# First retention outputs read while the last pair of gate columns is computed: loads, splits, stores and SBUF places around the start of the sliding-window phase

## The chip, the cores and the metric

The kernel runs on one core of one Trainium2 chip. Its engines work side by side, each in the order of its own queue: TensorE (PE, matmuls into PSUM), VectorE (DVE), ScalarE (ACT), GpSimd (POOL) and SyncE (SP), which only issues DMAs here. ACT and POOL can issue DMAs too. The metric is the device time of one execution in microseconds (us). Before the change the median of three runs is 2251.56 us.

## The reference

One layer of a streaming encoder over 1024 prompt tokens and 64 sample tokens, 1088 in all, with 1024 channels. What matters here is the first sublayer:

```python
rq, rk, rv, rg, sq, sk, sv, ga, gb = in_proj(h, g_attn, w_in)
...  # retention -> ret_o, sliding-window attention -> swa_o
a = (rms_norm(ret_o).astype(ret_g.dtype).reshape(B, S, -1) * jax.nn.silu(ret_g)) @ w_ret_out
b = swa_o.reshape(B, S, -1) @ w_swa_out
return (jax.nn.sigmoid(gate_a) * a + jax.nn.sigmoid(gate_b) * b) @ w_mix_out
```

`gate_b` (the columns `w_gb`) is the last thing that the projection computes. Then come the sliding-window attention (SWA: 16 query heads in 2 groups, a window of own chunk and two earlier chunks of 64 tokens) and the product with `w_ret_out`. Cross attention, a SwiGLU and a last norm follow, and the caches are returned.

## The kernel before

**Precision.** Every large product takes float32 operands split in two: a cast on ACT gives the high part, a subtraction on DVE the low part (`split`, L122 to L124), and three matmuls use them. Work that is "split" therefore always costs one ACT and one DVE instruction.

**Projection with seven products.** The projection handles two blocks of 128 output columns and both halves of the tokens at once (`strassen`, L247). For each such pair the weights `P1` to `P7` are made from two raw tiles (POOL adds, then splits into `wq` tiles, five of them), and PE runs seven products with the operands in the order `B11`, `B21`, `T2`, `T1`, `T3`, `B22`, `T4`. The operands live for the whole projection in two rings of eight slots of [128, 2, 1088] words each: ring 0 holds the two tiles of `T4` in slots 0 and 1, eight half-size staging areas in slots 2 and 3, `B11` in 4 and 5, `T1` in 6 and 7; ring 1 holds `B21` in 0 and 1, `B22` in 2 and 3, `T2` in 4 and 5, `T3` in 6 and 7. After the last pair each slot comes free when its product has been computed. The last pair's results are staged in ring 0's slot 3, the pair's before it in slot 2.

**Gate columns** (`project`, L654 to L664). For each result a DVE multiplication, an ACT sigmoid (L572) and a store into `d_gate` follow. For the swish gate (index 0, which then holds the gated retention outputs) the store is on SP, for the branch gates A and B (indices 1, 2) on ACT's own queue (L658). During most pairs a piece of the memory keys and values is computed as well.

**SWA phase** (`swa`, L871, with `filler`, L1045). A query chunk of 64 tokens and half of the heads make one step; 34 steps are run as a software pipeline in the order weigh, scores, turn (transposes), and between them pieces of dense work from `filler`: four pieces of the last memory values (`w_mv`) and then, for each of eight column blocks of `w_ret_out`, six pieces of 12 matmuls (three token chunks of 384, 384 and 320 columns, each in two halves of the contraction). PE's order is written out by hand (`in_order`). All other engines get their order from a scheduler that simulates the program: instructions traced earlier, or under `high_priority`, go first among those whose inputs and space are ready by its own model. `issue_after(x)` keeps an instruction behind `x` on the same engine's queue.

**Space in SWA.** The eight slots of ring 0 are taken anew as `swin` tiles, from slot 4 on: `flat[0]`, `flat[1]` are `B11`'s, `flat[2]`, `flat[3]` `T1`'s, `flat[4]`, `flat[5]` `T4`'s, `flat[6]`, `flat[7]` the staging areas'. They hold kT and vT (keys and values, 128 x 1216 words), the bias (128 x 1536), two buffers of queries (128 x 2048, for four chunks each), transposed values `vts`, and ten load buffers of 384 columns, `lds`. In ring 1 eight `ret` tiles take the split retention outputs. `operands` (L1055) loads them from `d_gate[0]` chunk by chunk of the tokens, eight loads of 128 x 384 (or 320) a chunk, through `lds`, and splits each. Their loads go on SP behind the `w_mv` loads. The loads of vT go behind the last load of the first chunk (`operand_loaded`), and the second query load (`load_queries(qTs, 4)`) is traced with the first scores. The raw tiles of `w_mv` (two) and of `w_ret_out` share two buffers.

## Time and profile before

| | us |
|---|---|
| runs, median (lowest to highest) | 2251.56 (2247.32 to 2252.81) |
| profiled execution, its own time | 2246.01 |
| its span, first to last instruction | 2244.2 |
| PE busy in the span | 2161.9 |
| mean granted PE clock | 0.988 of full |

A page of the profile shows one execution. Lines such as L123 name a line of the kernel, often that of a helper, so the tiles after it (`ret<-swin`) tell what it works on. "Idle before" an instruction is the time in which its engine had nothing to do, and what ended it. In the timeline views a row has the start, the length, engine, line, operation, output and input tiles and, in brackets, that idle time. DMA issues show on the issuing queue (SPq, ACTq); they land later.

### The profile page before, as it was taken

To read this page: it belongs to the slowest core of one execution; us is meant where nothing else is said; L and a number is where in the kernel's file an instruction comes from. 1 tells how busy PE (TensorE), PEld (TensorE's weight loads), DVE (VectorE), ACT (ScalarE), POOL (GpSimd) and SP (SyncE) were. 2 spreads that over 40 slices of the span, in tenths; PEclk is the share of its full clock that TensorE was granted. 3 is DMA by queue.
4 is the path that set the end of the run, shared out by engine and by line. 5 is a ranking of instruction groups with operands and counts; after the bars stand their busy time and mean duration, and the time that the engine had idled before them with its cause. 6 is when DMAs were issued, how large, how long until landed. Compare 5 with 4: busy or idle time off the path is not lost.

```text
span 2244.2 us, 41644 instructions
## 1 busy us (share of the span) xinstructions
PE 2161.9 (96%) x16374; PEld 2097.0 (93%) x16374; DVE 1602.8 (71%) x2655; ACT 883.9 (39%) x1896; POOL 689.8 (31%) x466
## 2 busy tenths in 40 slices
PE   7899999999999989999999999999999999999996
PEld 6899999999999977779999998999999999999986
DVE  8995878676687568875455565676777777778587
ACT  7333333435444355553233343333222222344343
POOL 1441533342263112220000000015555556434462
PEclk9999999999999989999999999999999999999998
DMA  5433345443545475327343112422342332476233
GB/s 198 161 116 110 111 130 134 130 127 115 172 141 188 144 242 166 111 68 219 118 153 119 38 49 71 133 78 88 122 138 92 102 128 83 151 263 196 75 96 108
DMA packets 182598, 290.84 MB, mean 130 GB/s; under 512 B 40290, under 2 KB 110850, under 8 KB 182402
## 3 DMA queue, kind: packets, MB, share of 16 engines
q1 hardware_dynamic: 177794, 279.26, 39.2%
q10 hardware_dynamic: 4608, 8.91, 1.1%
q8 instruction: 129, 2.11, 0.4%
q14 instruction: 67, 0.55, 0.1%
HBM read 196.95 MB, written 91.16 MB: 128 GB/s over the span
## 4 chain that ended last, share of the span: by engine, by line
PE 80%; DVE 10%; DMA 4%; issue 2%; ACT 2%; POOL 1%; SPq 0%; DVEq 0%; ACTq 0%; POOLq 0%
PE pq L208 15%; PE pq L205 15%; PE pq L206 15%; PE pd L149 8%; PE pd L151 8%; PE pd L150 8%; DVE wq L124 2%; PE pout L992 1%; DMA hl<-d_op 1%; PE pp L976 1%; PE pss L934 1%; DVE T L124 1%; DVE B L124 1%; DMA qs<-d_qkv 1%; PE pk L691 1%
## 5 line engine op out<-in xcount | busy, mean ns | idle before, releaser
L124 DVE TENSOR_TENSOR wq<-raw,wq 128x512 fp32r<-128x512 f32 (+1 forms) x505 | 456.6, 908 | 126.4 <-ACT wq L123 124.2
L123 ACT CAST wq<-raw 128x512 fp32r<-128x512 f32 (+1 forms) x505 | 307.7, 614 | 562.6 <-PE pq L208 266.5
L205 PE MATMUL pq<-T,wq 128*128 128x272 f32 x1832 | 492.5, 289 | 5.6 <-DVE u L252 3.7
L206 PE MATMUL pq<-T,wq 128*128 128x272 f32 x1832 | 492.8, 289 | 0.0
L206 PE MATMUL pq<-B,wq 128*128 128x272 f32 x1592 | 430.1, 290 | 9.7 <-DVE B L124 9.5
L205 PE MATMUL pq<-B,wq 128*128 128x272 f32 x1592 | 428.0, 289 | 11.8 <-ACT wq L123 10.6
L208 PE MATMUL pq<-T,wq 128*128 128x272 f32 x1832 | 384.1, 290 | 3.6 <-DVE wq L124 3.6
L183 POOL TENSOR_TENSOR raw<-raw 128x512 f32<-128x512 f32 (+1 forms) x59 | 82.7, 1402 | 905.9 <-DVE wq L124 623.6
L205 PEld LDWEIGHTS pq<-T,wq 128*128 128x128 f32 x1832 | 346.0, 189 | 6.3 <-DVE u L252 3.7
L206 PEld LDWEIGHTS pq<-T,wq 128*128 128x128 f32 x1832 | 346.0, 189 | 0.3 <-issue 0.3
L208 PE MATMUL pq<-B,wq 128*128 128x272 f32 x1592 | 334.2, 290 | 0.0
L206 PEld LDWEIGHTS pq<-B,wq 128*128 128x128 f32 x1592 | 301.2, 189 | 12.2 <-DVE B L124 11.8
L205 PEld LDWEIGHTS pq<-B,wq 128*128 128x128 f32 x1592 | 300.8, 189 | 12.5 <-ACT wq L123 10.6
L208 PEld LDWEIGHTS pq<-T,wq 128*128 128x128 f32 x1832 | 291.0, 190 | 5.1 <-DVE wq L124 4.4
L208 PEld LDWEIGHTS pq<-B,wq 128*128 128x128 f32 x1592 | 253.5, 190 | 0.5 <-issue 0.3
L252 DVE TENSOR_TENSOR u<-pq,u 128x544 f32<-128x544 f32 x177 | 127.5, 721 | 112.3 <-PE pq L208 111.7
L186 POOL TENSOR_TENSOR raw<-raw 128x512 f32<-128x512 f32 (+1 forms) x59 | 83.1, 1408 | 133.8 <-DVE wq L124 126.2
L563 DVE TENSOR_TENSOR stage<-pq,u 128x544 f32<-128x544 f32 x112 | 80.3, 717 | 27.7 <-PE pq L208 25.3
L962 POOL TENSOR_TENSOR t<-t,den 128x768 f32<-128x768 f32 (+2 forms) x34 | 47.9, 1407 | 167.4 <-DVE nm L950 58.7
L184 POOL TENSOR_TENSOR raw<-raw 128x512 f32<-128x512 f32 (+1 forms) x59 | 88.1, 1494 | 3.7
L189 POOL TENSOR_TENSOR raw<-raw 128x512 f32<-128x512 f32 (+1 forms) x59 | 84.0, 1424 | 4.4
L1438 POOL TENSOR_TENSOR y<-u,y 128x544 f32<-128x544 f32 x38 | 61.9, 1638 | 76.3 <-DVE y L1436 52.0
(370 smaller groups left out, 4647.2 us busy)
## 6 DMA issues: line engine op xcount, KB each, us to landing
hl<-d_op SPq DMA_DIRECT2D x85, 272.0 KB, 4.0
d_qkv<-stage SPq DMA_DIRECT2D x44, 272.0 KB, 2.1
d_op<-stage SPq DMA_DIRECT2D x44, 272.0 KB, 2.1
d_op<-ht SPq DMA_DIRECT2D x44, 272.0 KB, 3.2
raw<-w_gate SPq DMA_DIRECT2D x22, 512.0 KB, 3.4
raw<-w_up SPq DMA_DIRECT2D x22, 512.0 KB, 3.6
d_gate<-stage ACTq DMA_DIRECT2D x32, 272.0 KB, 2.3
raw<-w_down SPq DMA_DIRECT2D x16, 512.0 KB, 4.4
```

Of the source, the lines that this page charges most:

```text
L123: self.last_cast = self.nc.scalar.copy(hi, src).ins
L124: return self.nc.vector.tensor_tensor(out=lo, in0=src, in1=hi.bitcast(F32), op=ALU.subtract).ins
L149: mm(ps, wh, xh, start=start, stop=False)
L150: mm(ps, wh, xl, start=False, stop=False)
L151: self.last_mm = mm(ps, wl, xh, start=False, stop=stop).ins
L184: tt(out=a21, in0=a21, in1=a22, op=add)
L186: tt(out=a11, in0=a22, in1=a11, op=sub)
L189: tt(out=a12, in0=a12, in1=a11, op=sub)
L205: mm(ps[:, c, :HC], w[:, 0, ks], x[:, 0, cs], start=start, stop=False)
L206: mm(ps[:, c, :HC], w[:, 0, ks], x[:, 1, cs], start=False, stop=False)
L208: self.last_mm = mm(ps[:, c, :HC], w[:, 1, ks], x[:, 0, c * HC:(c + 1) * HC], start=False, stop=stop).ins
L252: add = lambda out, a, b: nc.vector.tensor_tensor(out=out, in0=a, in1=b, op=ALU.add)
```

## The change

Five things change. The last pair of gate B columns stores its four results by GpSimd's queue. The `swin` tiles get new uses: kT goes from `B11`'s first slot to `T1`'s first, the bias to `T1`'s second, the transposed values to the staging slot 2, and the load buffers to `B11`'s first slot (five at first) and `T4`'s second (five more after the first chunk). The eight `ret` tiles are put into ring 1's slots in the order `B21`, `T2`, `T3`, `B22`. The first chunk's operand loads no longer have to be behind the `w_mv` loads, and the later chunks' and vT's go behind the bias load; the second query load goes behind the last operand load. The first unit of `w_ret_out` is loaded and split ahead of the second chunk in the order of tracing.

```diff
-                    store = nc.scalar.dma_start if idx else self.store
+                    store = nc.gpsimd.dma_start if (idx, m) == (2, KT - 2) else nc.scalar.dma_start if idx else self.store
...
-            kT, vT = flat[0][:, :KC], flat[5][:, :KC]
-            bias = flat[2][:, :NPAIR * NKEY].rearrange("p (a b) -> p a b", b=NKEY)
+            kT, vT = flat[2][:, :KC], flat[4][:, :KC]
+            bias = flat[3][:, :NPAIR * NKEY].rearrange("p (a b) -> p a b", b=NKEY)
...
-            vts = [flat[4][:, i * P:(i + 1) * P] for i in range(17)] + [flat[0][:, KC + i * P:KC + (i + 1) * P] for i in range(3)]
-            self.lds = [t[:, i * 384:(i + 1) * 384] for t in (flat[3], flat[6]) for i in range(5)]
+            vts = [flat[6][:, i * P:(i + 1) * P] for i in range(17)] + [flat[2][:, KC + i * P:KC + (i + 1) * P] for i in range(3)]
+            self.lds, self.more_lds = ([t[:, i * 384:(i + 1) * 384] for i in range(5)] for t in (flat[0], flat[5]))
...
-                    self.load(bias[e * 64:(e + 1) * 64], src)
+                    self.bias_loaded = self.load(bias[e * 64:(e + 1) * 64], src)
...
-                if hf == 0 and c % 4 == 0 and c + 4 < 17:
+                if hf == 0 and c % 4 == 0 and 0 < c < 13:
                     self.load_queries(qTs, c + 4)
...
-                    with tc.high_priority(), tc.issue_after(self.operand_loaded):
+                    with tc.high_priority(), tc.issue_after(self.bias_loaded):
                         tokens(vT, 1, "cvT")
+                    with tc.issue_after(self.last_operand):
+                        self.load_queries(qTs, 4)
...
-            rets = self.ring_tiles(1, KT, "ret")
+            rets = [self.rings[1].tile(f"ret{k}", slot=i) for k, i in enumerate((0, 1, 4, 5, 6, 7, 2, 3))]
 
             def operands(c0, n):
-                after = self.loaded
+                after = self.bias_loaded
                 for k in range(KT):
                     a = ld()
-                    with tc.issue_after(after):
-                        ins = self.load(a[:, :n], self.d_gate[0][k, :, c0:c0 + n])
-                    if c0 == 0:
-                        self.operand_loaded = ins
+                    with tc.issue_after(after) if c0 else nullcontext():
+                        self.last_operand = self.load(a[:, :n], self.d_gate[0][k, :, c0:c0 + n])
                     self.split(a[:, :n], rets[k][:, 0, c0:c0 + n], rets[k][:, 1, c0:c0 + n])
-
-            for c0, n in CH:
+                if c0 == 0:
+                    self.lds += self.more_lds
+
+            operands(*CH[0])
+            first = self.unit(io["w_ret_out"][0], KT)
+            for c0, n in CH[1:]:
                 operands(c0, n)
...
-                u = self.unit(io["w_ret_out"][m], KT)
+                u = self.unit(io["w_ret_out"][m], KT) if m else first
```

More of the change, by code (lines that the diff above doesn't have):

```diff
@@ L1 @@
 import math
-from contextlib import ExitStack, contextmanager
+from contextlib import ExitStack, contextmanager, nullcontext
 import numpy as np
```

## The prediction

> **What bounds the kernel now.** I read the page first.

> ```profile
> span 2244.2 us, 41644 instructions
> PE 2161.9 (96%) x16374; PEld 2097.0 (93%) x16374; DVE 1602.8 (71%) x2655; ACT 883.9 (39%) x1896; POOL 689.8 (31%) x466
> ```

> TensorE (PE) is busy for 96% of the span, so a change that touches no matmul can only win where PE stands idle or runs at a lowered clock. The busy times by stage show one such place around this change, the seam between the last pair of gate columns and the sliding-window (SWA) phase; the columns are busy us (and instructions) of PE, PEld, DVE, ACT and POOL, then granted PE clock, DMA share and GB/s.

> ```profile
> 800.00:814.20 14.20, 14.20 (x116) 14.05 (x115) 6.29 (x10) 1.97 (x3) 0.00 (x0) 1.00 0.79 228
> 814.20:817.50 3.30, 0.57 (x8) 0.43 (x8) 1.45 (x2) 1.28 (x3) 0.00 (x0) 0.84 0.52 164
> 817.50:823.30 5.80, 5.61 (x24) 5.32 (x25) 5.04 (x13) 5.71 (x16) 0.00 (x0) 0.51 0.92 294
> 826.10:830.00 3.90, 2.40 (x23) 1.58 (x22) 2.92 (x10) 1.69 (x9) 0.00 (x0) 1.00 0.91 317
> 830.00:835.10 5.10, 0.00 (x0) 0.00 (x0) 3.60 (x12) 5.10 (x21) 1.81 (x2) 0.51 0.91 321
> 835.10:838.00 2.90, 2.23 (x6) 1.73 (x7) 2.90 (x6) 2.90 (x7) 0.13 (x1) 0.50 1.00 322
> 838.00:841.00 3.00, 3.00 (x14) 2.18 (x14) 2.83 (x6) 1.75 (x6) 0.00 (x0) 0.62 0.88 263
> 852.30:862.00 9.70, 9.70 (x74) 7.65 (x72) 9.08 (x20) 6.66 (x27) 2.97 (x2) 1.00 0.66 205
> 814.20:852.30 38.10, 25.85 (x162) 21.30 (x162) 31.09 (x76) 27.00 (x85) 3.79 (x4) 0.78 0.90 291
> 862.00:999.00 137.00, 137.00 (x976) 106.34 (x976) 109.39 (x241) 71.71 (x275) 36.69 (x25) 1.00 0.31 97
> ```

> From 814.2 to 852.3 PE is idle for 38.1 - 25.85 = 12.25 us. Before it and from 862 on PE never idles, so what the seam gives up should reach the end one for one. The same seam has DMA at 0.90 of its time and DVE at 31.09 of 38.1. The timeline of PE names what ended the largest gaps; in brackets stands the idle time:

> ```profile
> 817.55 0.58 PE L149 MATMUL pd<-wq,ms 128*128 128x256 f32 x1 [2.78 <-ACT wq L123]
> 829.65 0.33 PE L911 MATMUL pd<-ident,swin 128*128 128x128 f32 x1 [0.80 <-DMA swin<-d_skv]
> 835.14 0.69 PE L149 MATMUL pd<-ret,wq 128*128 128x384 f32 x1 [5.16 <-ACT wq L123]
> 836.77 0.69 PE L151 MATMUL pd<-ret,wq 128*128 128x384 f32 x1 [0.62 <-DVE wq L124]
> ```

> The chain of waits (start, us, what) says why the longest lasts until 835:

> ```profile
> 816.42 0.36 ACTq L658
> 816.94 0.46 issue
> 817.40 1.65 ACT wq L123 x3
> ...
> 820.13 8.16 DMA swin<-d_gate
> 828.31 0.51 ACT ret L123
> ...
> 838.48 6.59 DMA raw<-w_ret_out
> ```

> ACT, in order, sits on the eighth load of a retention output (issued at 820.13, and landed 8.16 us later) with the casts of the first `w_ret_out` unit behind it. SyncE's (SP) queue shows why loads are late:

> ```profile
> 794.79 0.32 SPq L117 DMA_DIRECT2D swin<-d_skv  x1
> ...
> 796.29 0.37 SPq L117 DMA_DIRECT2D swin<-d_sq  x1
> 797.80 3.23 SPq L117 DMA_DIRECT2D raw<-w_mv  x2
> 803.75 1.32 SPq L117 DMA_DIRECT2D swin<-d_rb  x2
> 806.92 12.68 SPq L117 DMA_DIRECT2D swin<-d_gate  x7
> 819.70 0.38 SPq L117 DMA_DIRECT2D swin<-d_sq  x1
> ```

> The space of operand `B11` comes free first (kT goes into it at 794.79), that of `T1` only around 803.75 (the bias goes into it); the load buffers lie behind that. At 819.70 a query load (`d_sq`) stands ahead of the eighth operand load.

> **The change, part by part.** (1) The load buffers take the `B11` tile, so five operand loads can start at 794.8 instead of 806.9, and three more as the first splits free a buffer; the `ret` tiles are numbered by the order in which the products free ring 1 (`B21`, `T2`, `T3`, `B22`). Products end 3.0 us apart, as their evacuations show (805.25, 808.24):

> ```profile
> 805.25 0.72 DVE L252 TENSOR_TENSOR u<-pq,u 128x544 f32<-128x544 f32 x1 [2.26 <-PE pq L208]
> 808.24 0.72 DVE L252 TENSOR_TENSOR u<-pq,u 128x544 f32<-128x544 f32 x1 [2.26 <-PE pq L208]
> ```

> So the eight slots come free between about 798 and 811, and eight casts and eight subtractions fit ahead of 814.2. Their prices in the seam, by group (count, busy us, mean ns):

> ```profile
> L124 DVE TENSOR_TENSOR ret<-swin,ret 128x384 fp32r<-128x384 f32 x16 | 9.6, 629 | 1.6 <-ACT ret L123 1.5
> L123 ACT CAST ret<-swin 128x384 fp32r<-128x384 f32 x16 | 7.3, 507 | 3.5 <-DMA swin<-d_gate 3.5
> ```

> Eight cost DVE 9.6 / 2 = 4.8 us and ACT 7.3 / 2 = 3.7 us. In 800 to 814.2 DVE is busy 6.29 and ACT 1.97 of 14.2, so they lie beside PE at no cost. If that cover failed (a cast waiting on a late load with the evacuation of a product behind it) PE would stop once its three result buffers are full, two products or 6 us later.

> (2) kT moves behind `T1`, from 794.8 to about 803.6, beside the bias at about 805. Bytes that have to land from 794.8 until the first retention matmul, by the shapes of the tiles: kT 0.6 MB, queries 1.05, `w_mv` 1.05, bias 0.8, eight operands 1.57, stores 1.1, vT 0.6, `w_ret_out` 0.5, and up to 1.57 of the next chunk ahead of it: 8.9 MB. At the seam's 291 GB/s that is 30.6 us (until 825.4), at the 334 GB/s of the row below (797.0 to 803.7) 26.6 us.

> ```profile
> DMA packets 1111, 2.24 MB, mean 334 GB/s; under 512 B 206, under 2 KB 334, under 8 KB 1110
> ```

> PE gets to that matmul at about 828.7 (after 826.1 come 2.40 us of work and some 0.7 of a wait between two score tiles, less 0.5 from part 4), so the 5.16 us should go. What could be late next is `w_ret_out`, whose raw buffer is free only after the `w_mv` splits (about 819).

> (3) vT waits for the bias load only, the second query load goes behind the last operand load, `w_ret_out` ahead of the second chunk. That removes the 0.80 us (vT) and 0.62 us (DVE), and SP's stop at 819.70.

> (4) Four stores leave ACT's queue for POOL's. ACT's casts of `w_mv` come 0.5 us earlier (0.36 issue and part of the 0.46 behind it), PE's first gap shrinks from 2.78 to 2.3 us. POOL is idle there:

> ```profile
> 824.87 0.77 POOL L962 TENSOR_TENSOR t<-t,den 128x256 f32<-128x256 f32 x1 [28.85 <-ACT ret L123]
> L658 ACTq DMA_DIRECT2D d_gate<-stage x6: 326/326/359, 781.2 to 816.4; - x6
> DMA to landing us min/median/max: 2.0/2.5/4.8
> ```

> The trace has no store issued by POOL. From below I bound its cost by ACT's 0.33 us and 2.0 us landing, from above by SP's slowest operand load (0.50 us to issue, 8.16 to land). Either way the last lands by 816.4 + 8.7 = 825. Only the second query load waits for it (the gate columns are read much later), and that load comes up on SP after all operand loads; the 16 later ones alone carry 2.9 MB, 8.7 us at 334 GB/s, so hardly before 823. I take nothing; at the upper bound SP stands for 2 us, with later `w_ret_out` units behind it that PE needs six pieces later.

> (5) Clock. After the 5.16 us gap PE runs at 0.50 and 0.62. The work of 835.1 to 841.0 at full clock is 2.23 x 0.50 + 3.00 x 0.62 = 3.0 us of 5.9, so 2.9 us, of which 0.6 is the DVE gap counted above: 2.3 us.

> **Sum** on PE: 5.16 + 0.80 + 0.62 + 0.5 + 2.3 = 9.4 us at most. DVE caps it: 31.09 - 4.8 = 26.3 us of work take 32.2 us at its present share (0.82), 28.1 at the 0.94 of 852.3 to 862: 5.9 to 10.0 us won. DMA too: 38.1 x 291 = 11.1 MB less 1.57 takes 32.7 us at 291 GB/s, 28.5 at 334: 5.4 to 9.6 won. I take 8.0, the middle of DVE's bounds, since DVE is the busiest engine of the seam and its work is what the later steps wait for. The profiled execution took 2246.0 (span 2244.2 and 1.8 around it), 5.6 below the median of the runs shown, so 2238.0 of it means 2251.6 - 8.0 = 2243.6 of the median.

> **The rivals.** (A) The wait only moves: the same bytes are carried by a DMA system busy 0.90 of the seam, and ACT meets the second chunk or `w_ret_out` (the 6.59 us row) where it met the first. Then only 0.5 + 0.8 + 0.6 = 1.9 us remain, 2249.7. For it speaks the DMA share of 0.91 to 1.00 from 817.5 to 838; against it that DMA is at 0.52 from 814.2 to 817.5 and can be filled.

> (B) The first gap no longer halves the clock. Now 817.5 to 823.3 runs at about 0.50 after 2.78 us of idling; with 2.3 us it might stay full, 5.8 / 2 = 2.9 us more, 2240.7. Against it: the clock already fell to a mean of 0.84 within 814.2 to 817.5.
> [...]

> (C) Slower: SP's queue is in order, and kT's three loads are written ahead of the operands with high priority. If they are also ahead in SP's queue, SP stands at them from 794.8 to 803.6 and every load behind them, queries and `w_mv` too, starts up to 8.8 us later, the chain at 820.13 with them. Price 0 to 8.8 us; with the full price and the 1.9 us of A, 2251.6 + 8.8 - 1.9 = 2258.5. It decides from the first load SP issues after 794.8. Against it: at 806.92 seven operand loads stand ahead of a query load written before them whose buffer wasn't free; for it: bias and operands do keep their written order.

> **How the numbers follow.** Forecast 0.57 (own range 2241 to 2247), A 0.20, B 0.10, C 0.13. A measurement of this kernel tells about 0.3% (6.8 us, below 2244.8) from no change. Of the forecast's chance 0.7 lies beyond that: faster 0.40 + 0.10 = 0.50; same 0.17 + 0.20 = 0.37; slower 0.13. The range reaches down to a gain near all that the seam loses (12.25 idle plus half-clock work, some 15 us) and up into C's smaller prices: 2236 to 2254.

> **What would show it.** Operand loads on SP from 794.8 on, eight `ret` casts before 814; the first `ret` matmul near 829 at clock 1.00 with no wait over 1 us; steady PE from about 844 in place of 852; the first gap still there, then 0.50. It is wrong if kT leads SP's queue, if PE has idle time before 814, or if ACT waits on an operand or `w_ret_out` load for 3 us or more after 817.

## The result, and the profile after

| | kernel before | changed kernel |
|---|---|---|
| runs on the same chip, median (lowest to highest), us | 2249.18 (2245.82 to 2255.40), 14 runs | 2256.12 (2252.99 to 2261.21), 14 runs |
| ratio, 95% interval | 1 | 1.0032 (1.0024 to 1.0040) |
| profiled execution, its own time, us | 2246.01 | 2259.77 |

The change makes the kernel slower by 0.32%, 6.9 us of the medians; 2243.6 had been predicted, 8 us faster. The profiled execution of the changed kernel is 13.8 us longer than that of the kernel before, more than the medians say, so the two traces must be cut into stretches before they are compared. These are the header lines of its page:

```profile
span 2258.0 us, 41646 instructions
...
PE 2168.5 (96%) x16374; PEld 2104.1 (93%) x16374; DVE 1600.3 (71%) x2655; ACT 885.4 (39%) x1896; POOL 689.6 (31%) x470
```

As marks I take PE's and DVE's timelines: the last evacuation of the gate columns (L563), the first `ret` matmul, the first 320-column piece of the first `w_ret_out` unit, the last `ret` matmul, the first `swa` matmul (where the merge begins) and the first `xc` matmul after the merge. The table has us from the first mark, one profile in each line:

| | L563 at | first ret | first 320 | last ret | first swa | first xc |
|---|---|---|---|---|---|---|
| before | 814.22 | 20.92 | 42.72 | 219.74 | 219.89 | 413.88 |
| changed | 816.92 | 14.59 | 42.04 | 219.08 | 226.18 | 419.81 |
| changed, second profile | 814.39 | 13.49 | 39.89 | 216.93 | 223.89 | 416.94 |

Three readings follow. The 2.70 us before the first mark lie in code that the change does not touch, and the second profile does not have them. From the end of the merge on the order of work is the same too, and the span left after the last `co` matmul (in the cross attention) is 749.7 to 756.1 us in the thirteen profiles whose marks stand above and below (750.9 before, 756.1 after, 751.5 in the second profile). So of the 13.8 us, 2.7 lie ahead of the first mark and 5.2 behind the merge, in code that both kernels share, and 5.9 between (419.81 against 413.88). What belongs to the change is between: the seam, which wins 0.7 us (2.8 in the second profile) where 8 were forecast, and the step from the last `ret` to the first `swa` matmul, which costs 7.0 us (219.08 to 226.18, against 219.74 to 219.89).

**The seam.** PE's timeline of the changed kernel, only rows with a wait over 0.5 us (idle time in brackets):

```profile
819.65 0.39 PE L149 MATMUL pd<-wq,ms 128*128 128x256 f32 x1 [2.18 <-ACT wq L123]
...
829.98 0.71 PE L934 MATMUL pss<-swin,swin 64*128 64x128 f32 x8 [1.67 <-DVE t L947]
...
842.99 1.06 PE L976 MATMUL pp<-ident,t 128*64 128x128 f32 x4 [6.38 <-POOL t L962]
```

The waits of 0.80, 5.16 and 0.62 us are gone. A new one of 6.38 us stands at the transposes of half (0,1), which need `t` from POOL. The busy times in three stretches (same columns as in the prediction) show the price, PE idle for 6.49 of 15 us and a granted clock of 0.68, while DVE is busy 13.46 of 15:

```profile
815.00:830.00 15.00, 10.81 (x82) 10.08 (x80) 9.52 (x23) 9.63 (x24) 1.69 (x3) 0.89 1.06 306
830.00:845.00 15.00, 8.51 (x45) 7.00 (x46) 13.46 (x40) 13.61 (x48) 1.93 (x3) 0.68 0.94 317
845.00:860.00 15.00, 15.00 (x94) 11.86 (x93) 9.29 (x20) 5.84 (x22) 2.26 (x2) 0.87 0.55 190
```

DVE's timeline says what it was busy with. DVE's part of the half's softmax is the chain L949, L950, L951, L954, L959, L960 on rows of 4 elements; splits (L124) stand between its links:

```profile
830.82 0.41 DVE L949 TENSOR_REDUCE nm<-t 128x4 f32<-128x256 f32 x1
831.15 1.48 DVE L124 TENSOR_TENSOR ret<-swin,ret 128x384 fp32r<-128x384 f32 x3
...
833.22 0.15 DVE L950 TENSOR_TENSOR nm<-nm,sinks 128x4 f32<-128x4 f32 x1
833.28 1.35 DVE L124 TENSOR_TENSOR ret<-swin,ret 128x384 fp32r<-128x384 f32 x3
...
835.22 1.28 DVE L124 TENSOR_TENSOR wq<-raw,wq 128x512 fp32r<-128x512 f32 x2
...
837.56 0.15 DVE L954 TENSOR_TENSOR es<-sinks,nm 128x4 f32<-128x4 f32 x1
...
840.55 0.89 DVE L124 TENSOR_TENSOR ret<-swin,ret 128x320 fp32r<-128x320 f32 x2
...
841.98 0.17 DVE L960 RECIPROCAL den<-den 128x4 f32<-128x4 f32 x1
```

Between 830.82 and 841.98 the engine rests for 0.16 us only, but the splits of the third chunk (128x320) and of the next two `w_ret_out` units are work that PE needs only later, and PE stands for the softmax behind them. ACT's half of each split does the same. The exponentials of the half are done at 837.7 and `es` (L954) is ready at 837.71, but ACT takes it up only at 839.79, behind casts, the first of which had to wait for its load:

```profile
837.49 0.19 ACT L956 ACTIVATION_READ_ACCUMULATOR t<-t,nm 128x1 f32 x1
838.03 1.14 ACT L123 CAST wq<-raw 128x512 fp32r<-128x512 f32 x2 [0.35 <-DMA raw<-w_ret_out]
839.07 0.81 ACT L123 CAST ret<-swin 128x320 fp32r<-128x320 f32 x2
839.79 0.20 ACT L958 ACTIVATE es<-es 128x4 f32<-128x4 f32 x1
```

**The merge.** PE's timeline there has one wait (the second row is the same matmul in the kernel before, without one), and the windows behind it a lowered clock:

```profile
1043.10 1.33 PE L149 MATMUL pd<-swa,wq 128*128 128x384 f32 x3 [6.79 <-ACT swa L123]
```

```profile
1034.11 0.34 PE L149 MATMUL pd<-swa,wq 128*128 128x384 f32 x1
```

```profile
1036.00:1043.00 7.00, 0.31 (x3) 0.04 (x1) 4.60 (x9) 3.83 (x9) 0.00 (x0) 0.80 0.97 321
1043.00:1048.00 5.00, 4.90 (x18) 4.90 (x19) 3.75 (x9) 3.05 (x8) 0.00 (x0) 0.60 0.90 269
```

`merge_swa` retakes ring 0's slots for eight tiles `swa0` to `swa7`, from slot 4 on. So `swa0` lies where `flat[0]` was. The change puts load buffers there, and these serve until the last `d_mix` stores of the SWA phase. Every accumulation of the merge begins with k = 0, so the tile that comes free last is now the one needed first. In the kernel before, the load buffers in use at the end lay in `flat[6]`, which becomes `swa6`, and PE worked on the six tiles ahead of it without a gap.

### The profile page after: what moved, and what is told of

Its sections match the earlier page's. It is cut to its first block, busy times and chain, and to the rows that moved or that the text cites. A ratio compares the mean times of both kernels' runs of the same rounds, so it can differ in the third digit from the quotient of the medians.

```text
span 2258.0 us, 41646 instructions
## 1 busy us (share of the span) xinstructions
PE 2168.5 (96%) x16374; PEld 2104.1 (93%) x16374; DVE 1600.3 (71%) x2655; ACT 885.4 (39%) x1896; POOL 689.6 (31%) x470
## 4 chain that ended last, share of the span: by engine, by line
PE 79%; DVE 10%; DMA 4%; issue 3%; ACT 2%; POOL 1%; SPq 0%; DVEq 0%; ACTq 0%; POOLq 0%
PE pq L208 15%; PE pq L206 15%; PE pq L205 15%; PE pd L149 7%; PE pd L151 7%; PE pd L150 7%; DVE wq L124 2%; PE pout L992 2%; PE pp L976 1%; PE pss L934 1%; DMA hl<-d_op 1%; DVE B L124 1%; DVE stage L563 1%; DVE T L124 1%; DMA ld<-d_swa 1%
## 5 line engine op out<-in xcount | busy, mean ns | idle before, releaser
L124 DVE TENSOR_TENSOR wq<-raw,wq 128x512 fp32r<-128x512 f32 (+1 forms) x505 | 452.6, 900 | 127.2 <-ACT wq L123 125.3
L123 ACT CAST wq<-raw 128x512 fp32r<-128x512 f32 (+1 forms) x505 | 307.6, 614 | 566.7 <-PE pq L208 276.1
L208 PE MATMUL pq<-T,wq 128*128 128x272 f32 x1832 | 383.9, 290 | 3.4 <-DVE wq L124 3.4
L208 PE MATMUL pq<-B,wq 128*128 128x272 f32 x1592 | 335.5, 291 | 0.0
L208 PEld LDWEIGHTS pq<-T,wq 128*128 128x128 f32 x1832 | 291.1, 190 | 4.5 <-DVE wq L124 3.8
L208 PEld LDWEIGHTS pq<-B,wq 128*128 128x128 f32 x1592 | 254.9, 191 | 0.5 <-issue 0.3
L252 DVE TENSOR_TENSOR u<-pq,u 128x544 f32<-128x544 f32 x177 | 127.5, 720 | 107.3 <-PE pq L208 106.6
L563 DVE TENSOR_TENSOR stage<-pq,u 128x544 f32<-128x544 f32 x112 | 80.3, 717 | 25.4 <-PE pq L208 22.8
L962 POOL TENSOR_TENSOR t<-t,den 128x768 f32<-128x768 f32 (+2 forms) x34 | 47.4, 1393 | 146.0 <-DVE nm L950 51.3
```

The lines of the kernel that those rows point to most:

```text
L123: self.last_cast = self.nc.scalar.copy(hi, src).ins
L124: return self.nc.vector.tensor_tensor(out=lo, in0=src, in1=hi.bitcast(F32), op=ALU.subtract).ins
L208: self.last_mm = mm(ps[:, c, :HC], w[:, 1, ks], x[:, 0, c * HC:(c + 1) * HC], start=False, stop=stop).ins
L252: add = lambda out, a, b: nc.vector.tensor_tensor(out=out, in0=a, in1=b, op=ALU.add)
L563: nc.vector.tensor_tensor(out=o, in0=ps, in1=sb, op=ALU.add)
```

## The experiments

All ratios are to the kernel before, with 95% intervals. e1 to e5 shared runs of it (median 2249.9), then e3c, e7, e6 and the second profile (2248.64), then e9, e8 and e6_again (2249.27). Their marks, in us from the last evacuation as above:

| | first ret | first 320 | last ret | first swa | first xc |
|---|---|---|---|---|---|
| e1_swap | 13.41 | 39.38 | 216.31 | 216.45 | 410.38 |
| e2_before_swap | 20.93 | 42.00 | 219.08 | 226.37 | 420.11 |
| e3b_order | 13.96 | 35.08 | 256.88 | 257.03 | 451.02 |
| e3c_splits | 14.17 | 36.43 | 220.89 | 221.03 | 414.96 |
| e9_third | 13.26 | 36.03 | 213.07 | 213.21 | 407.20 |
| e5_actstore | 17.61 | 43.12 | 220.03 | 220.17 | 414.09 |
| e6_unfirst | 16.00 | 37.75 | 214.68 | 214.83 | 408.75 |
| e6_again | 16.00 | 39.70 | 216.74 | 216.89 | 410.87 |
| e7_wfirst | 13.68 | 37.84 | 221.27 | 221.41 | 415.33 |
| e8_third_unfirst | 13.67 | 40.31 | 217.40 | 217.54 | 411.53 |

### e1_swap and e2_before_swap: the place of `swa0`

Both have one line of the merge altered, e1 in the changed kernel and e2 in the kernel before; `swa0` and `swa6` exchange their slots:

```diff
-            swas = self.ring_tiles(0, KT, "swa")
+            swas = [self.rings[0].tile(f"swa{k}", slot=i) for k, i in enumerate((2, 5, 6, 7, 0, 1, 4, 3))]
```

> The changed kernel with one line of the merge altered: swa0 and swa6 exchange their places in ring 0, so that swa6, not swa0, retakes the last-used load buffers (flat[0]). Theory M (the place of the load buffers makes swa0, with which all three accumulations of the merge begin, the last operand to be ready): the 6.79 us wait of TensorE at the first swa matmul (1043.10 in the changed kernel's profile) goes, the half clock behind it too, and the time falls by 6 to 7 us to about 2249.5, level with the kernel before. Rival D (the swa loads themselves land late in the changed kernel, whatever tile they go to): the wait stays above 5 us and the time stays at about 2256. Rival S (the loss is in the seam at 815 to 853, or spread over later stages): the wait may go, but the time stays above 2254.

> The kernel before with the same line of the merge altered: there the last-used load buffers lie in flat[6], and the exchange puts swa0 into them. Theory M: the kernel before gets the wait of the changed kernel, 5 to 8 us of TensorE at the first swa matmul with a lowered clock behind it, and the time grows by 6 to 7 us to about 2256. Rivals D and S: no wait above 2 us there and a time within 2 us of the kernel before.

Measured: e1 2247.93 (2244.92 to 2251.2), ratio 0.9986 (0.9977 to 0.9995). e2 2257.75 (2254.41 to 2260.53), ratio 1.0034 (1.0023 to 1.0045). First e1's, then e2's row of PE's timeline:

```profile
1034.20 0.34 PE L149 MATMUL pd<-swa,wq 128*128 128x384 f32 x1
```

```profile
1041.80 1.33 PE L149 MATMUL pd<-swa,wq 128*128 128x384 f32 x3 [6.98 <-DVE swa L124]
```

In e1 the bracket is empty, in e2 the kernel before has the wait of the changed one. The loads of `d_swa` keep their order in both, so it is the place and not the data that is late. Theory M holds in both directions; by the ratios the exchange is worth 7.6 us in the kernel before (0.0034 x 2249) and about 10 in the changed one (0.0046 x 2249, interval 8 to 13, from ratios to two sets of runs), the wait itself 6.8 to 7.0. What the rest of the 10 us is, no run shows. The half clock behind the wait adds nothing that the marks show: from the first `swa` to the first `xc` matmul it takes 193.6 us in the changed kernel, 194.0 before.

### after_again: how far two profiles of one kernel agree

> The changed kernel once more, for its seam alone: from the last evacuation of the gate columns to the first 320-column piece it took 42.0 us in the first profile and 39.4 in e1_swap, whose code is the same up to there. If the 2.7 us are from execution to execution, this profile lies between 39 and 42.5; the merge's wait of about 6.8 us is there again in any case.

It ran in 2249.55 us, below all 14 runs of the changed kernel above; it is one run without a ratio, and I draw nothing from its time. The merge's wait is 6.66 us. The seam took 39.89 us to the first 320-column piece, inside the expected bounds, so 2 to 3 us of the seam are from execution to execution, and single marks are to be read so.

### e3b_order, e3c_splits, e9_third: the order of DVE's and ACT's queues

e3b puts the splits of the third chunk's operands and of each later `w_ret_out` unit behind the last softmax traced before them (`exps` and `dens`, the `Exp` of `es` and the reciprocal: the casts go behind the first on ACT, the subtractions behind the second on DVE); e3c only the splits of the third chunk and of the second unit; e9 only those of the third chunk. In all three the third chunk is also traced later. The edit of e9 to e1, without the two lines that note these instructions:

```diff
+            @contextmanager
+            def softmax():
+                with tc.issue_after(self.exps), tc.issue_after(self.dens):
+                    yield
...
-                    self.split(a[:, :n], rets[k][:, 0, c0:c0 + n], rets[k][:, 1, c0:c0 + n])
+                    with softmax() if c0 == CH[2][0] else nullcontext():
+                        self.split(a[:, :n], rets[k][:, 0, c0:c0 + n], rets[k][:, 1, c0:c0 + n])
...
-            for c0, n in CH[1:]:
-                operands(c0, n)
+            operands(*CH[1])
...
+            operands(*CH[2])
```

The last line stands behind the four pieces of `w_mv`, so that the third chunk is traced after the scores of the first halves.

> e1_swap, and the splits of the third chunk's operands and of the later w_ret_out units are put behind the softmax of the halves traced before them on VectorE and ScalarE. Theory Q (the 6.38 us wait of TensorE for POOL's t at 842.99 comes from VectorE's in-order queue, in which splits that TensorE needs later stand ahead of the softmax of half (0,1)): the wait falls below 2 us, TensorE is steady from about 845 in place of 853, and the time falls by 4 to 5 us against e1_swap, to about 2245. Rival T (DMA sets the seam: the first w_ret_out unit and the second chunk land late, and the softmax waits on nothing else): a wait of 5 us or more remains, at a ret or w_ret_out operand in place of t, and the time stays within 1.5 us of e1_swap.

> e1_swap, with the splits of the third operand chunk and those of the second w_ret_out unit behind the softmax of the halves traced before them; the loads, and all later w_ret_out units, are left where e1_swap has them. Theory Q (from e3b_order: the seam was won by the order of VectorE's queue, and the 40 us were lost by holding every later w_ret_out unit behind a softmax far ahead): from the last evacuation of the gate columns to the first 320-column piece of the first w_ret_out unit it takes 35 to 36 us as in e3b_order (39.4 in e1_swap, 42.7 in the kernel before), the three waits of 4 to 5 us from 861 on are gone, and the time falls by 3 to 4 us against e1_swap, to about 2244. Rival R (the reordered splits of the third chunk are themselves what is late after the seam): waits of over 2 us at ret operands between 850 and 900 stay, and the time is above that of e1_swap.

> e1_swap, with the splits of the third operand chunk alone behind the softmax of the halves traced before them; the second w_ret_out unit is left where e1_swap has it (in e3c_splits it was moved too, and its cast ended a wait of 4.37 us at 863.96). Theory Q: the wait of TensorE for POOL's t (7.85 us in e1_swap) is below 3 us as in e3c_splits, the 4.37 us wait is gone, the time from the gate columns' last evacuation to the last ret matmul is 213 to 215 us (216.3 in e1_swap), and the time falls by 1 to 3 us against e1_swap. Rival R (the third chunk's splits are late after the seam): a wait of over 2 us at a ret operand between 845 and 870, and 217 us or more to the last ret matmul.

Measured: e3b 2287.86, ratio 1.0164 (1.0145 to 1.0182); e3c 2250.02, ratio 1.0005 (0.9993 to 1.0016); e9 2244.99 (2241.92 to 2248.99), ratio 0.9983 (0.9973 to 0.9994). In all three the seam shortens as theory Q said, from 39.4 in e1 to 35.1, 36.4 and 36.0 us, and the wait for `t` falls to 2.5 (7.85 in e1). The times expected of e3b and e3c, about 2245 and 2244 us, were missed all the same, because of what the edit makes late. In e3b PE waits for a `w_ret_out` unit six times from 855 us on, as its list of waits shows (us in total, times, longest):

```profile
PE pd L149 <- ACT wq L123: 30.8, 6, 5.3
```

e3c has one such wait. First PE's row, then ACT's from the same trace:

```profile
863.96 0.69 PE L149 MATMUL pd<-ret,wq 128*128 128x384 f32 x1 [4.37 <-ACT wq L123]
```

```profile
861.45 0.45 ACT L956 ACTIVATE t<-t,nm 128x192 f32<-128x192 f32 x1 [3.38 <-DVE nm L951]
...
863.31 2.16 ACT L123 CAST wq<-raw 128x512 fp32r<-128x512 f32 x4
```

ACT idles 3.38 us for a maximum of DVE with the unit's casts queued behind: a split put behind a softmax too far ahead is the same mistake with the roles changed. e9 leaves the unit alone. Its PE timeline and its windows:

```profile
836.84 0.62 PE L976 MATMUL pp<-ident,t 128*64 128x128 f32 x4 [2.51 <-POOL t L962]
...
841.00 0.65 PE L992 MATMUL pout<-pT,swin 64*64 64x256 f32 x4 [1.45 <-ACT pT L979]
```

```profile
815.00:830.00 15.00, 11.80 (x90) 11.07 (x91) 10.29 (x25) 10.66 (x28) 2.22 (x4) 0.89 1.06 333
830.00:845.00 15.00, 11.03 (x71) 8.94 (x69) 13.68 (x39) 12.43 (x46) 2.81 (x3) 0.90 0.96 305
845.00:860.00 15.00, 14.75 (x106) 11.78 (x105) 14.79 (x31) 8.23 (x32) 2.94 (x2) 0.99 0.70 218
```

From 830 to 845 DVE is as busy as in the changed kernel (13.68 against 13.46) and DMA as full (0.96, 0.94), but PE works 11.03 us in place of 8.51, at clock 0.90 in place of 0.68. So neither DVE's amount of work nor DMA's set the changed kernel's seam; the order of the work did. What part DVE's queue, ACT's queue and the loads have in it is not separated: a split has one instruction on each of the two engines, and the third chunk's first load, traced later, is issued at 829.84 in e9 and at 825.86 in e1. e9 is faster than both kernels: 0.9983 of the kernel before, against 1.0032 for the changed one. Against e1 it is 3.2 us shorter to the last `ret` matmul, where two profiles of the changed kernel differ by 2.1, and the two ratio intervals overlap, so a gain in time over e1 is not shown.

### e5_actstore: the stores back on ACT

e1 with the line of the change on the stores undone (`nc.scalar.dma_start if idx else self.store`).

> e1_swap with the last four stores of the gate columns back on ScalarE's queue (undoes part 4 of the change). The prediction's price for part 4: TensorE's first gap (2.18 us at 819.65 in the changed kernel) grows back by about 0.5 us to 2.7 and the time by 0.5 us, not to be told from e1_swap by the median. Rival G (the GpSimd stores hold up something: a later landing, the second query load): the time falls by over 2 us against e1_swap.

Measured: 2250.45 (2248.71 to 2255.22), ratio 1.0004 (0.9995 to 1.0014), and e1 0.9986 (0.9977 to 0.9995) on the same chip: the GpSimd stores are worth 0.0018 x 2249 = 4 us (interval 1 to 7), by the medians 2.5, not 0.5. ACT's part is as priced, the first gap is 2.69 us again. The rest is in SP's queue; its rows of e5, and its largest waits from 795 to 835 in the kernel before, in e5 and in e1:

```profile
809.14 4.33 SPq L117 DMA_DIRECT2D raw<-w_mv  x2
...
815.47 0.34 SPq L117 DMA_DIRECT2D swin<-d_skv  x1
819.00 0.33 SPq L117 DMA_DIRECT2D swin<-cvT  x1
823.22 0.33 SPq L117 DMA_DIRECT2D swin<-d_skv  x1
...
824.59 0.38 SPq L117 DMA_DIRECT2D raw<-w_ret_out  x1
```

```profile
SPq L117 <- DMA d_gate<-stage: 11.6, 4, 5.9
```

```profile
SPq L117 <- DMA d_gate<-stage: 10.7, 3, 3.9
```

```profile
SPq L117 <- PE pq L208: 6.8, 3, 5.1
SPq L117 <- DVE ret L124: 4.5, 6, 2.4
```

With the stores on ACT, SP stands 10.7 us at a load of `w_mv` and two of vT until stores have landed, although neither touches the other's tiles. In the kernel before, whose list has the same wait with 11.6 us, the four waits are those of the operand loads at 806.92, 813.14, 816.54 and 819.28. In that trace's records SP's loads and ACT's stores take turns on the same eight completion counters (100 to 104 and 106 to 108), and each of the four waits for the counter of one of ACT's stores: 104, 106, 107 and 102, of the stores at 802.03, 811.08, 813.43 and 816.42. In the changed kernel's records the stores issued by GpSimd count on others (111 to 114), and neither its list of waits nor e1's has such a wait.

### e6_unfirst, e6_again, e8_third_unfirst, e7_wfirst: where the first `w_ret_out` unit stands

e6 is e1 with `first` traced behind all three chunks again; e8 is e6 with e9's move; e7 is e3c with the second chunk's loads behind the first unit's load (`tc.issue_after(self.loaded)` for that chunk).

> e1_swap, with the first w_ret_out unit traced behind all three operand chunks again, as in the kernel before (undoes that piece of part 3). Theory of the prediction (the unit's load ahead of the second chunk lets TensorE reach the first ret matmul without a wait): the first ret matmul waits 3 us or more again, for ScalarE's cast of the unit, and the time grows by 0 to 3 us. Rival (the wait for POOL's t covers it): the wait only changes place, and the time stays within 1 us of e1_swap.

> e6_unfirst a second time, since its profile (5 us less than the kernel before from the gate columns to the merge) and its 12 timed runs (ratio 0.9993, interval 0.9982 to 1.0005) do not say the same. If the seam of the profile is the kernel's usual one, the ratio is 0.997 to 0.999; if the profile was a lucky execution, the ratio is 0.999 to 1.000 and the new profile shows 216 us or more to the last ret matmul.

> e6_unfirst with the same move of the third chunk's splits. e6_unfirst had no wait over 2.5 us left and 214.7 us to the last ret matmul. If VectorE's order is still what the seam waits for, this falls to 212 to 213.5 us; if the seam is now set by the sum of VectorE's work and the loads, it stays within 1 us of e6_unfirst, and the time too.

> e3c_splits, with the eight loads of the second operand chunk issued behind the load of the first w_ret_out unit. If the 7.12 us landing of that unit (820.95 in the changed kernel) is what holds the first ret matmul, it lands earlier and the time falls by another 1 to 2 us against e3c_splits; if the second chunk, split ahead of the softmax of half (0,1), is what the seam waits for, its later loads make the time grow by 1 to 4 us.

Measured: e6 2247.36, ratio 0.9993 (0.9982 to 1.0005), and 2246.97, 0.9992 (0.9984 to 1.0001); e8 2249.5, 1.0001 (0.9990 to 1.0013); e7 2252.84, 1.0015 (1.0005 to 1.0026). e6's PE timeline in the first of its two profiles:

```profile
827.10 1.22 PE L934 MATMUL pss<-swin,swin 64*128 64x128 f32 x8 [2.47 <-DVE t L947]
...
830.76 0.69 PE L149 MATMUL pd<-ret,wq 128*128 128x384 f32 x1 [1.19 <-ACT wq L123]
...
836.21 0.63 PE L976 MATMUL pp<-ident,t 128*64 128x128 f32 x4 [0.45 <-POOL t L962]
```

Without `first` ahead of the chunks the `ret` matmul comes 2.6 us later (16.0 against 13.4), after a wait of 1.19 us and not the 3 or more expected, but the wait for `t` is 0.45 us, and the two ratios can't be told from e1's. e6_again came out as its second branch: the same edit takes 216.74 us to the last `ret` matmul in place of 214.68, so the first profile was a lucky execution. That the early unit buys its 2.6 us by putting its splits ahead of the softmax fits this, but is not shown. e8 missed its 212 to 213.5 us; its wait for `t` has only moved to a later half:

```profile
852.39 1.11 PE L976 MATMUL pp<-ident,t 128*128 128x128 f32 x4 [6.48 <-POOL t L962]
```

e9, whose only difference is the early unit, has none over 2.6 (ratio 0.9983 against 1.0001). e7 can't be told from e3c by ratio (1.0015 against 1.0005, intervals overlapping): neither of its two branches is shown. Its waits moved to 844 and 852 us. I can't say beforehand which of these orders is best; that stays open.

## Why the prediction was wrong

**Part 1, first half: right.** Aligned by the 2.70 us at the first mark, operand loads start at 794.8 as said, kT behind them (so rival C is out, and that its 2258.5 us lies nearest to the 2256.1 measured is coincidence), and ACT casts all eight before the columns' end. SP's rows, and the group of casts from 795 to 815:

```profile
797.50 1.30 SPq L117 DMA_DIRECT2D swin<-d_gate  x3
...
799.40 5.85 SPq L117 DMA_DIRECT2D swin<-d_gate  x5
806.46 0.32 SPq L117 DMA_DIRECT2D swin<-d_skv  x1
```

```profile
L123 ACT CAST ret<-swin 128x384 fp32r<-128x384 f32 x8 | 4.1, 511 | 7.0 <-PE pq L208 4.9 <-DMA swin<-d_gate 2.1
```

The first `ret` matmul comes at 831.5 - 2.7 = 828.8, where 828.7 was predicted, and the 5.16 us wait is gone. That the two agree to 0.1 us is partly luck: the wait between the score tiles is 1.67 us in place of 0.7, and the clock behind the first gap 0.70 in place of 0.51. In the second profile and in e1 the matmul comes 1.1 and 1.2 us earlier.

**Part 1, second half: the failed step.** "The load buffers take the `B11` tile" was priced only by what could start earlier. Who takes `flat[0]` next, and when the load buffers give it up, was not asked; the trace of before held the answer (no wait at the first `swa` matmul, whose tiles are taken in the same order). The statement that what the seam gives up should reach the end one for one failed here: 7 us went at the merge. None of the signs of being wrong that were named came up (kT does not lead SP's queue, PE is busy without a gap from 785 to 817.4, ACT's longest wait for a `w_ret_out` load after 817 is 0.8 us), because all three looked at the seam.

**The sum: the second failed step.** PE was to be steady from 844. In the changed kernel's windows it is without a gap at full clock only from 850, that is 847 when aligned:

```profile
840.00:845.00 5.00, 2.02 (x8) 1.91 (x9) 3.62 (x15) 4.36 (x20) 1.93 (x3) 0.50 1.05 374
845.00:850.00 5.00, 5.00 (x24) 3.58 (x23) 1.35 (x3) 0.00 (x0) 0.76 (x1) 0.60 1.01 360
850.00:855.00 5.00, 5.00 (x36) 4.14 (x35) 3.23 (x7) 2.91 (x11) 0.00 (x0) 1.00 0.38 131
```

The sum capped PE's 9.4 us by DVE's busy share and so treated DVE's work as one amount. The engine kept pace (13.46 of 15 us busy) and PE still waited 6.38 us, because earlier operands brought later operands' splits ahead of a softmax. Part 5's 2.3 us for the clock went with it: behind the new wait the clock is 0.50 and 0.60 again. Rival A, a wait that only moves, was the seam's true case: 1.9 us forecast, 0.7 and 2.8 measured. Its 2249.7 us did not come, because of the merge. The wait moved to the softmax, too, and not to ACT's meeting with a late load (ACT stands 0.35 us for one there), and DMA, at 0.94 to 1.06 from 815 to 845, was no bound: e9 wins 6.7 us (219.74 to 213.07) at 0.96.

**Part 4: mis-sized.** The GpSimd stores cost nothing, as said (issued in 0.54 to 0.71 us each, landed after 6.6 in the median), and the first gap fell to 2.18 us (2.3 predicted). But their gain was put at 0.5 us, and it is 2.5 to 4. The prediction put the late operand loads of 806.92 to 819.70 down to their space; SP's list of waits, which it does not use, has 11.6 us for `d_gate<-stage` there.

**Part 3: not the gain it was taken for.** The 0.80 and 0.62 us went, but the early `w_ret_out` unit is worth nothing that e6 can show; together with e9's order it is worth 4 us by ratio (e8 against e9, 0.0018 x 2249).

## What to carry to other kernels

When a buffer moves, ask two questions of its new place: when it comes free for its new use, and who takes it next and when that user needs it; here the first tile of an accumulation inherited the last buffer in use, which cost 7 us. A load that comes earlier also brings its splits earlier into the queues of DVE and ACT, where PE's wait for a softmax behind them was 6.38 us here, so look at what is queued behind them before booking the wait as won. And read the issuing queue's own list of waits: a DMA issued from another engine can hold it up without sharing a byte, as SP was held up for 11.6 us in the kernel before.

## What the runs showed of the hardware

SP's loads stood 11.6 us in the kernel before for stores that another engine had issued. What stood behind a waiting load was issued later too: two of vT's three loads wait in e5, so that they stand at 815.47, 819.00 and 823.22, 3.5 and 4.2 us apart (815.41, 815.79 and 816.30 in the changed kernel), and the operand load behind them at 823.64 (816.86).

The clock behind one and the same first gap of 2.18 us came out three ways. These are the 5.8 us behind it in the changed kernel, in its second profile and in e3c:

```profile
819.65:825.40 5.75, 5.41 (x30) 5.21 (x31) 3.87 (x10) 4.25 (x13) 0.27 (x1) 0.70 1.04 365
```

```profile
817.13:822.90 5.77, 5.43 (x43) 5.23 (x44) 4.17 (x13) 4.80 (x15) 0.27 (x1) 1.00 1.04 391
```

```profile
819.09:824.90 5.81, 5.66 (x25) 5.37 (x26) 4.14 (x12) 4.33 (x13) 0.27 (x1) 0.50 1.04 385
```

The granted clock is 0.70, 1.00 and 0.50. After 2.78 and 2.75 us (the kernel before and e2) it was about 0.50 both times, after e5's 2.69 us it was 0.71. So the length of the gap alone does not decide, and rival B, a clock that stays full behind a shorter gap, is true of some executions and not of others.
